# The last four blocks of the down projection in three token parts of 288, 128 and 128 instead of two of 288 and 256

## The chip, the core and the metric

The kernel runs on one core of one Trainium2 chip. The metric is the device time of one execution in microseconds (us), from which a median over runs is taken. A NeuronCore has five engines that each follow their own list of instructions: TensorE (PE in the profile; its weight loads have a row of their own, PEld), VectorE (DVE), ScalarE (ACT), GpSimd (POOL) and SyncE (SP), and 16 DMA engines that move data between the memory of the chip and the on-chip memory. They meet through semaphores.

## What is computed

One inference step of a decoder layer for 512 prompt tokens and 8 x 4 sample tokens, 544 columns in all. Only the end matters here:

```
x = x + (silu(conv) * (u @ w_up)) @ w_down
...
yp = rmsnorm(yp, norm_final)
ys = rmsnorm(ys, norm_final)
```

The rmsnorm divides each token by the root of the mean of its 1024 squares and multiplies by a gain. So no token's output can be formed before all eight row blocks of the down projection have been added for that token.

## The kernel before

Activations lie transposed: 1024 features are 8 tiles `x[m]` (m = 0 to 7, names `xr` in the profile) of 128 partitions, and the 544 tokens are the free dimension. A dense product is done as three products in fp32r (the function `passes`, line 829): every fp32 operand is split into a high and a low part, and high x high, high x low and low x high are added in PSUM. Each of the three has weights of 128 x 128 that are loaded anew. In the feed-forward network the hidden width of 2816 makes 22 blocks; the down projection over blocks 0 to 17 is woven into the products of the gate and the up projection, and blocks 18 to 21 (`DOWN_LAST`, line 39) come at the end, when nothing else is left for TensorE. This end is what the change touches.

There the tokens are cut by `LAST_CUTS` (line 57) in two parts, c = 0 with 288 tokens and c = 1 with 256. `last_half(m, c)` (line 2289) makes one row block m of part c: 4 blocks x 3 products = 12 products into a PSUM tile `ps_dz`, then VectorE adds it to `x[m]`, ScalarE squares the sum, and the square is added to a running sum `acc_final` by GpSimd (m = 1 to 5) or VectorE (m = 6); for m = 0 the square is the running sum's start, and for m = 7 it is kept apart in `sq_last`. For the m in `ON_POOL[c]` ScalarE also multiplies the sum by the gain into `y`. `final(c)` (line 2308) makes the norm of a part: two plain fp32 products with a matrix of ones (`psr_final`) sum the squares over the partitions, ScalarE takes Ln and two Exp (one into PSUM for VectorE, `r_final`; one into `r_fin` for GpSimd), VectorE or GpSimd form eight tiles `y`, and eight DMAs write them out. The order of calls is all of part 0, then part 1 with `final(0)` behind its block m = 2, then `final(1)`.

Nothing is issued as written. The class `Tape` (line 252) records all instructions as steps, and its `order` (line 434) plays them through with its own lengths and lags to fix each engine's list; what stands under `tape.main()` keeps its order on TensorE. PSUM tiles `ps_dz` rotate through three banks (`PF`, line 675), those of the norm through five others (`PX`, line 672). In the profile every recorded compute instruction has line 642, and every DMA line 617, since a helper issues them; the two files differ by one line there, so the changed kernel has 643 and 618.

Of the kernel before, what the change touches and what calls it, by code (L numbers as in the profile page):

```python
# [22 lines left out]
KT = D // 128  # L23
# [9 lines left out]
LN_SET = "natural_log_exp_and_others"  # L33

PLAIN = 4

DOWNS = ((0, 4, 1, (1, 1, 1, 1)), (4, 8, 5, (1, 1, 1, 1)), (8, 12, 9, (1, 1, 1, 1)), (12, 16, 13, (1, 1, 1, 1)),
         (16, 18, 15, (1, 1, 1, 1)))
# [15 lines left out]
LAST_MV = 4  # L54
CUTS = ((0, 256), (256, 288))

LAST_CUTS = ((0, 288), (288, 256))

TILES = (2, 2, 1)
PAIR_LEAD = 10.0  # L60
# [586 lines left out]
def tile_decoder_step(ctx: ExitStack, tc: tile.TileContext, xT, memT, kwT, vw, s0, conv_in, mkT, mv, vecs, cst,  # L647
                      w_first, w_in, w_out, w_cq, w_ck, w_cv, w_co, w_gate, w_up, w_down,
                      yT, kT_out, vT_out, st_out, conv_out, mkT_out, mv_out, ss_out):
    nc = tape = Tape(tc.nc)  # L650
# [9 lines left out]
    def A(name, shape=None, dt=F32):  # L660
        return tape.tile(act, shape or [128, FW], dt, tag="a", name=name, bufs=NA)
# [10 lines left out]
    def PX(name):  # L672
        return tape.tile(psum, [128, 512], F32, tag="aux", name=name, bufs=5)

    def PF(name):

        turn[0] += 1
        return PDEC(name) if turn[0] % 3 == 0 else PD(name)
# [18 lines left out]
    def V(name, i=0):  # L697
        return vec[:, VEC_COLS[name][0] + i:VEC_COLS[name][0] + i + 1]

    def C(name):  # L700
        lo, hi = CST_COLS[name]
        return cs[:, lo:hi] if hi <= mid else cs2[:, lo - mid:hi - mid]
# [13 lines left out]
    ffn_w = len(specs)  # L716
    for j in range(PLAIN):
        specs += [w_gate[j], w_up[j]]
# [110 lines left out]
    def passes(ps, w, xs, n0, n, order, first=True, last=True):  # L829
        for at, i in enumerate(order):  # L830
            (hi, lo), (xh, xl) = w[i], xs[i]
            for j, (a, b) in enumerate(((hi, xh), (hi, xl), (lo, xh))):
                nc.tensor.matmul(ps[:, :n], a, b[:, n0:n0 + n], start=(first and at == 0 and j == 0),
                                 stop=(last and at == len(order) - 1 and j == 2))
# [876 lines left out]
    def add_to(m):  # L1711
        def evac(ps, n0, n):
            nc.vector.tensor_tensor(x[m][:, n0:n0 + n], x[m][:, n0:n0 + n], ps[:, :n], op=ALU.add)
        return evac
# [337 lines left out]
    def down_group(k0, k1, deps):  # L2052

        halves = []
        for m in range(KT):
            k = k1 - k0
            load, box = load_a(f"wd{k0}_{m}", w_down[m][:, 128 * k0:128 * k1].rearrange("p (k c) -> p k c", c=128), k)
            low = split_a(f"wd{k0}_{m}", box, k, load)
            halves += [down_half(k0, k1, m, c, (low, box), deps) for c in range(2)]
        return halves  # L2060
# [163 lines left out]
    gates, hids = {}, {}  # L2224
    for q in range(2 * PLAIN):
        kind, j = "gu"[q % 2], q // 2
# [7 lines left out]
    units = []  # L2234
    for j in range(PLAIN, FT, 2):
        for kind in "gu":
# [3 lines left out]
    downs = [(down_group(k0, k1, [hids[j] for j in range(k0, k1)]), first, each) for k0, k1, first, each in DOWNS]  # L2240
    seq = later.order[:4 * PLAIN]
    seq.insert(-1, units[0].q.pop(1))
# [36 lines left out]
    r_fin, last_sq = A("r_fin"), A("sq_last")  # L2279
    hs, k = [hid[j] for j in range(*DOWN_LAST)], DOWN_LAST[1] - DOWN_LAST[0]  # L2280
    ys = {}
    ON_POOL = (1, 3, 6), (1, 5)

    def y_at(m, c):
        if (m, c) not in ys:
            ys[m, c] = A(f"y{m}_{c}")
        return ys[m, c][:, :LAST_CUTS[c][1]]

    def last_half(m, c):
        n0, n = LAST_CUTS[c]  # L2290
        cut = slice(n0, n0 + n)
        if m == 0 and c == 1:
            tape.gate_at = len(tape.mains) - 1
            nc.sync.dma_start(conv_out, last2)
            nc.scalar.preload_act_table_set(LN_SET)
            tape.gate_at = None
        ps = PF(f"ps_dz{m}_{c}")
        with tape.main():
            passes(ps, held[m], hs, n0, n, range(k))
        add_to(m)(ps, n0, n)  # L2300
        if m < KT - 1:
            ssq3.add(x[m][:, cut], n0, nc.vector if m == KT - 2 else None)
        else:
            nc.scalar.activation(last_sq[:, cut], x[m][:, cut], AF.Square)
        if m in ON_POOL[c]:
            nc.scalar.activation(y_at(m, c), x[m][:, cut], AF.Copy, scale=V("norm_final", m))

    def final(c):
        n0, n = LAST_CUTS[c]
        cut = slice(n0, n0 + n)  # L2310
        ps = PX(f"psr_final{c}")
        for i, sq in enumerate((ssq3.acc, last_sq)):
            nc.tensor.matmul(ps[:, :n], C("ones"), sq[:, cut], start=i == 0, stop=i == 1)
        nc.scalar.activation(r_fin[:, cut], ps[:, :n], AF.Ln, bias=eps, scale=1.0 / D)

        r = PX(f"r_final{c}")[:, :n]
        nc.scalar.activation(r, r_fin[:, cut], AF.Exp, scale=-0.5)
        nc.scalar.activation(r_fin[:, cut], r_fin[:, cut], AF.Exp, scale=-0.5)
        for m in range(KT):
            out = y_at(m, c)  # L2320
            if m in ON_POOL[c]:
                nc.gpsimd.tensor_tensor(out, out, r_fin[:, cut], op=ALU.mult)
            else:
                nc.vector.scalar_tensor_tensor(out, x[m][:, cut], V("norm_final", m), r, op0=ALU.mult, op1=ALU.mult)
            (nc.scalar if c and m % 2 else nc.sync).dma_start(yT[128 * m:128 * m + 128, cut], out)

    held = []
    for m in range(KT):
# [5 lines left out]
            nc.vector.tensor_tensor(lo, t, hi.bitcast(F32), op=ALU.subtract)  # L2334
        held.append([(hi[:, i, :], lo[:, i, :]) for i in range(k)])
        last_half(m, 0)
    for m in range(KT):
        last_half(m, 1)
        if m == 2:
            with tape.main():  # L2340
                final(0)
    with tape.main():
        final(1)
    tape.run()


# [72 lines left out]
```

## Time and profile before

| | us |
|---|---|
| median of 3 runs | 826.87 (825.66 to 828.18) |
| the profiled execution's own time | 827.21 |
| its span, first to last instruction | 825.4 |
| TensorE busy in it | 813.9 (99%) |
| last product of the down projection starts | 816.45 |

The span is what the trace shows; some 1.8 us of the execution's time lie around it. Times in the trace count from the start of the span. TensorE's matmuls are pipelined: a row's duration (0.28 us for a product of 256 columns) is longer than the distance to the next one (0.12 us), and only the distances add up to time. The profile writes fp32r matmuls as f32 with x1 per product, and a plain fp32 product as two rows (x2), one per pass.

### The profile page before, as it was taken

How to read it: one execution, taken by the hardware profiler on the slowest of the kernel's cores; microseconds unless marked ns; L12 is line 12 of the kernel's file. 1: busy time of each engine (PE TensorE's matmuls, PEld its weight loads, DVE VectorE, ACT ScalarE, POOL GpSimd, SP SyncE). 2: the span in 40 equal slices, each digit the busy share in tenths (PEclk: the TensorE clock that was granted, in tenths of full speed). 3: DMA queues.
4: the chain of work that ended last, by engine and by line, in shares of the span. 5: the costliest groups of instructions: out<-in, count | busy, mean ns of one | idle time of the engine just before them, and what ended most of it. 6: DMA issues, size and time to landing. Idle time of an engine off the chain costs nothing.

```text
span 825.4 us, 18881 instructions
## 1 busy us (share of the span) xinstructions
PE 813.9 (99%) x7551; PEld 762.4 (92%) x7551; DVE 617.2 (75%) x1316; ACT 419.0 (51%) x835; POOL 148.0 (18%) x239
## 2 busy tenths in 40 slices
PE   9999999999999999999999999999999999999996
PEld 9999877887888889999889998999999999999995
DVE  6987889866879887564576998976777677767754
ACT  7643455434458345444545456554554455545533
POOL 0030211110210200222323131121112111211013
PEclk9999999999999999999999999999999999999999
DMA  9439999557823444260721347456456645653503
GB/s 343 156 121 297 352 287 304 166 170 226 289 81 110 158 145 153 59 218 31 256 86 53 103 103 203 130 131 176 118 140 181 139 116 145 163 149 83 164 1 109
DMA packets 90759, 132.32 MB, mean 160 GB/s; under 512 B 6064, under 2 KB 60080, under 8 KB 90544
## 3 DMA queue, kind: packets, MB, share of 16 engines
q1 hardware_dynamic: 84480, 120.69, 45.8%
q0 software_dynamic: 5184, 9.44, 7.2%
q8 instruction: 59, 0.97, 0.5%
q10 hardware_dynamic: 1008, 0.99, 0.4%
q14 instruction: 28, 0.23, 0.1%
HBM read 123.03 MB, written 8.07 MB: 159 GB/s over the span
## 4 chain that ended last, share of the span: by engine, by line
PE 91%; DVE 3%; ACT 2%; DMA 2%; issue 0%; SPq 0%; DVEq 0%; ACTq 0%
PE ps_d L642 13%; PE ps_au L642 6%; PE ps_ag L642 6%; PE ps_wo L642 6%; PE ps_cu L642 3%; PE ps_cg L642 3%; PE ps_z_v L642 3%; PE ps_co L642 3%; PE ps_g L642 3%; PE ps_cq L642 3%; PE ps_dz L642 3%; PE ps_u L642 3%; PE ps_z_g L642 2%; PE ps_z_i L642 2%; PE psdo L642 2%; PE psd L642 2%
## 5 line engine op out<-in xcount | busy, mean ns | idle before, releaser
L642 ACT CAST wh<-wr 128x1024 fp32r<-128x1024 f32 (+1 forms) x60 | 52.5, 889 | 73.6 <-issue 12.9
L642 DVE TENSOR_TENSOR wl<-wr,wh 128x1024 fp32r<-128x1024 f32 (+1 forms) x60 | 63.1, 1064 | 9.2 <-ACT wh L642 8.6
L642 DVE TENSOR_TENSOR xr<-xr,ps_d 128x256 f32<-128x256 f32 x80 | 34.5, 434 | 37.6 <-PE ps_d L642 37.5
L642 POOL COPY last<-ug 128x2 f32<-128x2 f32 (+1 forms) x44 | 14.7, 366 | 160.9 <-DVE ug L642 133.9
L642 DVE SCALAR_TENSOR_TENSOR cv<-ug,vec,cv 128x560 f32<-128x560 f32 x44 | 35.1, 798 | 8.1 <-ACT cv L642 7.8
L642 POOL TENSOR_TENSOR hG<-hG,z_f 128x256 f32<-128x256 f32 (+1 forms) x21 | 18.9, 899 | 118.9 <-DVE kq L642 63.5
L642 ACT ACTIVATE cv<-cv 128x560 f32<-128x560 f32 x22 | 14.8, 673 | 19.9 <-DVE cv L642 19.9
L642 ACT ACTIVATE cv<-ug,vec 128x560 f32<-128x560 f32 x22 | 18.8, 856 | 10.6 <-DVE ug L642 9.7
L617 POOL DMA_DIRECT2D S1u<-in_w_up x9 | 7.8, 862 | 89.4 <-DMA S1u<-in_w_up 45.3
L642 ACT ACTIVATE P<-P,mx 128x128 f32<-128x128 f32 (+3 forms) x32 | 17.7, 553 | 11.9 <-DVE mx L642 11.8
L642 POOL TENSOR_TENSOR acc_cx<-acc_cx,sq_cx 128x256 f32<-128x256 f32 (+1 forms) x14 | 11.4, 819 | 59.1 <-ACT sq_cx L642 59.0
L642 POOL COPY ug<-conv_state 128x16 f32<-128x16 f32 x22 | 18.4, 837 | 4.9 <-PE ps_u L642 2.8
L642 PE MATMUL ps_co<-coh,wh 128*128 128x256 f32 (+1 forms) x64 | 19.0, 297 | 0.0
L642 PE MATMUL ps_co<-coh,wl 128*128 128x256 f32 (+1 forms) x64 | 18.4, 288 | 0.0
L642 PE MATMUL ps_co<-col,wh 128*128 128x256 f32 (+1 forms) x64 | 18.4, 288 | 0.0
L642 POOL COPY qbd_win<-z_q 64x32 f32<-64x32 f32 x8 | 8.2, 1024 | 51.1 <-DVE z_q L642 50.9
L642 DVE TENSOR_TENSOR xr<-xr,ps_wo 128x256 f32<-128x256 f32 (+1 forms) x16 | 6.8, 435 | 13.9 <-PE ps_wo L642 13.8
L642 PE MATMUL psdo<-st,dpt 128*32 128x256 f32 x224 | 16.4, 386 | 0.0
L642 DVE TENSOR_TENSOR xr<-xr,ps_dz 128x288 f32<-128x288 f32 (+1 forms) x16 | 7.0, 436 | 12.3 <-PE ps_dz L642 12.3
L642 POOL TENSOR_TENSOR acc_ux<-acc_ux,sq_ux 128x256 f32<-128x256 f32 (+1 forms) x14 | 11.7, 834 | 20.9 <-ACT sq_ux L642 20.8
L642 PE MATMUL psd<-st,qbd_win 128*32 128x224 f32 x256 | 15.3, 358 | 0.0
L642 ACT ACT_TABLE_LOAD x11 | 14.1, 1283 | 2.3 <-issue 2.2
(3122 smaller groups left out, 3635.0 us busy)
## 6 DMA issues: line engine op xcount, KB each, us to landing
st<-in_kwT SPq DMA_DIRECT2D x32, 448.0 KB, 6.2
st<-in_vw SPq DMA_DIRECT2D x28, 512.0 KB, 5.7
wr<-in_w_in SPq DMA_DIRECT2D x17, 512.0 KB, 6.4
wd<-in_w_down SPq DMA_DIRECT2D x32, 256.0 KB, 2.8
wrg<-in_w_gate SPq DMA_DIRECT2D x9, 512.0 KB, 5.9
wru<-in_w_up SPq DMA_DIRECT2D x9, 512.0 KB, 4.6
st<-in_mkT SPq DMA_DIRECT2D x8, 512.0 KB, 6.8
wr<-in_w_out SPq DMA_DIRECT2D x8, 512.0 KB, 3.8
```

The costliest lines, as they stand in the source:

```text
L617: return tape.put(engine, lambda: call(*args, **kw), outs, ins, 0.1, 0.3, size)
L642: return tape.put(engine, lambda: call(*args, **kw), outs, ins, length, lag, size, port, words)
```

## The change

`LAST_CUTS` gets three parts: 288, 128 and 128 tokens. Part c = 1 and part c = 2 are each made of eight row blocks, and `final(c - 1)` follows block m = 2 of part 1 and block m = 4 of part 2 (`FINAL_AT`); `final(2)` is the last. `ON_POOL` gets a middle entry, and the outputs of the odd m of the last part alone go through ScalarE's DMA queue, so that the eight of the middle part go through SyncE's.

```diff
--- before.py
+++ after.py
@@ -33,6 +33,7 @@
 LN_SET = "natural_log_exp_and_others"
 
 PLAIN = 4
+FINAL_AT = 2, 4
 
 DOWNS = ((0, 4, 1, (1, 1, 1, 1)), (4, 8, 5, (1, 1, 1, 1)), (8, 12, 9, (1, 1, 1, 1)), (12, 16, 13, (1, 1, 1, 1)),
          (16, 18, 15, (1, 1, 1, 1)))
@@ -54,7 +55,7 @@
 LAST_MV = 4
 CUTS = ((0, 256), (256, 288))
 
-LAST_CUTS = ((0, 288), (288, 256))
+LAST_CUTS = ((0, 288), (288, 128), (416, 128))
 
 TILES = (2, 2, 1)
 PAIR_LEAD = 10.0
@@ -2279,7 +2280,7 @@
     r_fin, last_sq = A("r_fin"), A("sq_last")
     hs, k = [hid[j] for j in range(*DOWN_LAST)], DOWN_LAST[1] - DOWN_LAST[0]
     ys = {}
-    ON_POOL = (1, 3, 6), (1, 5)
+    ON_POOL = (1, 3, 6), (1, 4, 6), (1, 5)
 
     def y_at(m, c):
         if (m, c) not in ys:
@@ -2322,7 +2323,7 @@
                 nc.gpsimd.tensor_tensor(out, out, r_fin[:, cut], op=ALU.mult)
             else:
                 nc.vector.scalar_tensor_tensor(out, x[m][:, cut], V("norm_final", m), r, op0=ALU.mult, op1=ALU.mult)
-            (nc.scalar if c and m % 2 else nc.sync).dma_start(yT[128 * m:128 * m + 128, cut], out)
+            (nc.scalar if c == 2 and m % 2 else nc.sync).dma_start(yT[128 * m:128 * m + 128, cut], out)
 
     held = []
     for m in range(KT):
@@ -2334,13 +2335,14 @@
             nc.vector.tensor_tensor(lo, t, hi.bitcast(F32), op=ALU.subtract)
         held.append([(hi[:, i, :], lo[:, i, :]) for i in range(k)])
         last_half(m, 0)
-    for m in range(KT):
-        last_half(m, 1)
-        if m == 2:
-            with tape.main():
-                final(0)
+    for c in (1, 2):
+        for m in range(KT):
+            last_half(m, c)
+            if m == FINAL_AT[c - 1]:
+                with tape.main():
+                    final(c - 1)
     with tape.main():
-        final(1)
+        final(2)
     tape.run()
```

How this moves the instructions is seen in each engine's list. First TensorE before, at the end of the program: `ps_dz_1_...` are PSUM tiles of part 1 (the last number is the buffer's), `h21h` and `h21l` the parts of the hidden block, `wdhz`, `wdlz` those of the weights, `psr_final` the sum of squares.

```order
L642 MATMUL ps_dz_1_2030<-h21h,wdlz_1997 128x256
L642 MATMUL psr_final_2032<-acc_final,cs 128x288
L642 MATMUL psr_final_2032<-sq_last,cs 128x288
L642 MATMUL ps_dz_1_2039<-h18h,wdhz_2001 128x256
...
L642 MATMUL ps_dz_1_2048<-h21h,wdlz_2024 128x256
L642 MATMUL psr_final_2049<-acc_final,cs 128x256
L642 MATMUL psr_final_2049<-sq_last,cs 128x256
```

And TensorE's list at the same place in the changed kernel.

```order
L643 MATMUL ps_dz_1_2030<-h21h,wdlz_1997 128x128
L643 MATMUL psr_final_2032<-acc_final,cs 128x288
L643 MATMUL psr_final_2032<-sq_last,cs 128x288
...
L643 MATMUL ps_dz_2_2058<-h21h,wdlz_2008 128x128
L643 MATMUL psr_final_2060<-acc_final,cs 128x128
L643 MATMUL psr_final_2060<-sq_last,cs 128x128
L643 MATMUL ps_dz_2_2067<-h18h,wdhz_2012 128x128
...
L643 MATMUL ps_dz_2_2072<-h21h,wdlz_2024 128x128
L643 MATMUL psr_final_2073<-acc_final,cs 128x128
L643 MATMUL psr_final_2073<-sq_last,cs 128x128
```

Before, 8 x 12 products of 256 columns followed part 0; now 16 x 12 products of 128 columns do, with as many weight loads, and one more pair `psr_final` stands between the fifth and the sixth block of the last part.

Second, VectorE at the end of the changed kernel, from the sixth block of the last part on (`xr` is the addition to `x[m]`, `y_1` and `y_2` are outputs of the middle and the last part).

```order
L643 TENSOR_TENSOR xr_884<-xr_884,ps_dz_2_2067 128x128
L643 SCALAR_TENSOR_TENSOR y_1_2062<-xr_879,vec,r_final_2061 128x128
L643 SCALAR_TENSOR_TENSOR y_1_2063<-xr_881,vec,r_final_2061 128x128
L643 SCALAR_TENSOR_TENSOR y_1_2064<-xr_882,vec,r_final_2061 128x128
L643 TENSOR_TENSOR xr_885<-xr_885,ps_dz_2_2070 128x128
L643 SCALAR_TENSOR_TENSOR y_1_2065<-xr_884,vec,r_final_2061 128x128
L643 SCALAR_TENSOR_TENSOR y_1_2066<-xr_886,vec,r_final_2061 128x128
L643 TENSOR_TENSOR xr_886<-xr_886,ps_dz_2_2072 128x128
L643 TENSOR_TENSOR acc_final<-acc_final,sq_final_6_2071 128x128
L643 SCALAR_TENSOR_TENSOR y_2_2075<-xr_879,vec,r_final_2074 128x128
```

The five outputs of the middle part that VectorE makes stand ahead of the last two additions; before, all six of the last part came after them, 256 wide. Outside the end the planner's run differs in three places by a swap of neighbours (for one, two `psr_hg` products on TensorE).

## The prediction

> **What bounds the kernel now.** I read the page first: busy shares and the chain that ended last.
>
> ```profile
> PE 813.9 (99%) x7551; PEld 762.4 (92%) x7551; DVE 617.2 (75%) x1316; ACT 419.0 (51%) x835; POOL 148.0 (18%) x239
> PE 91%; DVE 3%; ACT 2%; DMA 2%; issue 0%; SPq 0%; DVEq 0%; ACTq 0%
> ```
>
> TensorE is busy for 99% of the span and carries 91% of the chain, so a product added anywhere before the last one moves the end by its full spacing. The end itself is another stage. The view by windows, cut at the moments that the timeline gives, shows it (columns: window, length, busy time and count of PE, PEld, DVE, ACT, POOL, granted clock, DMA share, GB/s).
>
> ```profile
> 804.24:808.50 4.26, 4.26 (x39) 4.26 (x38) 1.49 (x4) 1.77 (x5) 0.27 (x1) 1.00 0.01 4
> 808.50:809.58 1.08, 1.08 (x7) 0.87 (x6) 0.42 (x1) 0.42 (x2) 0.46 (x1) 1.00 0.00 0
> 809.58:816.57 6.99, 6.99 (x61) 6.95 (x59) 3.96 (x10) 3.48 (x9) 5.21 (x7) 1.00 0.49 169
> 816.57:819.36 2.79, 1.56 (x6) 0.59 (x4) 0.61 (x3) 1.28 (x4) 0.00 (x0) 1.00 0.00 0
> 819.36:823.95 4.59, 0.00 (x0) 0.00 (x0) 2.44 (x6) 0.41 (x1) 1.41 (x2) 0.75 0.68 228
> 823.95:825.40 1.45, 0.00 (x0) 0.00 (x0) 0.00 (x0) 0.00 (x0) 0.00 (x0) 0.50 0.00 1
> ```
>
> Up to 816.57 the second part's products run without a gap on TensorE at clock 1.00; then 8.83 us follow (825.40 - 816.57): 2.79 for the norm, 4.59 for outputs and their transfers, 1.45 of closing. The change shortens pieces of the 8.83 and doubles the number of products ahead of it. So two prices decide: a product of 128 columns, and the tail.
>
> **The products.** TensorE's timeline gives the spacing (start, duration, then the instruction):
>
> ```profile
> 802.66 0.29 PE L642 MATMUL ps_dz<-h18h,wdhz 128*128 128x288 f32 x1
> ...
> 804.24 0.28 PE L642 MATMUL ps_dz<-h18h,wdhz 128*128 128x256 f32 x1
> ...
> 808.50 0.65 PE L642 MATMUL psr_final<-acc_final,cs 128*128 128x288 f32 x2
> ...
> 816.45 0.28 PE L642 MATMUL ps_dz<-h21h,wdlz 128*128 128x256 f32 x1
> ```
>
> Twelve products of 288 columns take 804.24 - 802.66 = 1.58 us, 0.132 each; 36 of 256 take 808.50 - 804.24 = 4.26, 0.118 each. Were 128 columns priced by that slope (0.42 ns a column), one would cost 0.065. But each product also loads its 128 x 128 weights, and here 4.26 us of PE hold 4.26 us of PEld: the loads run all the time, hidden behind the columns. What a load costs when nothing hides it is seen where very few columns pass:
>
> ```profile
> 303.47 1.94 PE L642 MATMUL psds<-cs,domn 128*128 128x16 f32 x16
> 422.55 1.85 PE L642 MATMUL ps_cos<-cs,com 128*128 128x16 f32 x16
> L642 PE MATMUL psds<-cs,domn x16: 262/262/263, 303.5 to 305.1; 128*128 128x16 f32 x16
> L642 PEld LDWEIGHTS psds<-cs,domn x16: 192/192/192, 303.4 to 305.1; 128*128 128x128 f32 x16
> L642 PEld LDWEIGHTS ps_dz<-h18h,wdhz x16: 187/188/192, 791.4 to 815.0; 128*128 128x128 f32 x16
> L642 PEld LDWEIGHTS psO<-PT,vt x160: 132/137/138, 136.2 to 281.5; 128*64 128x64 f32 x160
> ```
>
> Sixteen passes with only 16 columns span 1.94 and 1.85 us; less the last one's 0.262 that is 15 distances of 0.112 and 0.106 us. Sixteen columns cannot fill that; the weights do. These are plain fp32 weights; for fp32r the trace has no product under 256 columns, so its price at 128 must be bounded. A load of fp32r weights is recorded with 188 ns, the fp32 one with 192, one of half as many weight columns with 137: the fp32r load looks like the full fp32 one. The lower bound is the slope's 0.065 (no load price at all); the upper one, if loads bind, is the 0.118 of today, behind which a load already fits. I take **0.110**, the middle of the two fp32 rows, to which the recorded load times are nearest.
>
> [...]
>
> Sum on TensorE from 804.24 on. Before: 8 x 12 x 0.1184 = 11.37, and `psr_final` of part 0 with 0.96 (12.33 = 816.57 - 804.24, less 11.37). After: 16 x 12 x 0.110 = 21.12, the same 0.96, and one more pair `psr_final` of 128 columns, four fp32 passes of 0.11 = 0.44 (at most the 0.96 of the wide one). That is 22.52 against 12.33: **+10.19 us**.
>
> Waits do not come on top. A PSUM bank is free again when VectorE has added its block; TensorE gives it 1.32 us per block, close to the 1.42 of now, and VectorE is busy for 3.96 of 6.99 us in the third window. The new `psr_final` pair is queued ahead of three blocks, but its sums are due long before: the middle part ends five blocks, 6.6 us, earlier, and the square and addition chain behind the last block takes about 1.2 us now (816.57 to 817.69 in the tail below).
>
> **The middle part's norm and output.** After that pair, three blocks or 3.96 us of products remain. In them VectorE has five `y_1`, three or four additions, ScalarE an Ln, two Exp and four to five squares or copies, GpSimd four operations. Rows of 128 columns, GpSimd's 256-wide additions, and SyncE's issues:
>
> ```profile
> L642 DVE SCALAR_TENSOR_TENSOR hst<-hst,ftots,psu 128x128 f32<-128x128 f32 x32 | 8.7, 343 | 0.5 <-PE psu L642 0.5
> L642 DVE TENSOR_TENSOR htm<-htm 128x128 f32<-128x128 f32 x4 | 1.2, 289 | 0.1
> L642 POOL TENSOR_TENSOR acc_final<-acc_final,sq_final 128x256 f32<-128x256 f32 x5 | 3.7, 734 | 6.2 <-ACT sq_final L642 6.2
> L617 SPq DMA_DIRECT2D out_yT<-y x12: 332/390/414, 811.2 to 821.5; - x12
> ```
>
> VectorE: 5 x 0.343 + 4 x 0.289 = 2.9 us, under 3.96. Four GpSimd operations of half the width are below 4 x 0.734 = 2.9. So this work is covered; its eight DMA issues on SP (0.4 each, 3.2 us) end about 827.2, and the last part's first output comes near 829. It costs nothing; if the cover were gone, see the last rival.
>
> **The tail.** What follows the last product before the change, behind one row of part 0 at 288 columns:
>
> ```profile
> 804.98 0.45 ACT L642 ACTIVATE sq_last<-xr 128x288 f32<-128x288 f32 x1 [0.61 <-DVE xr L642]
> ...
> 816.77 0.42 DVE L642 TENSOR_TENSOR xr<-xr,ps_dz 128x256 f32<-128x256 f32 x1
> 817.23 0.42 ACT L642 ACTIVATE sq_last<-xr 128x256 f32<-128x256 f32 x1 [1.00 <-DVE xr L642]
> 817.69 0.30 PEld L642 LDWEIGHTS psr_final<-sq_last,cs 128*128 128x128 f32 x2 [0.59 <-ACT sq_last L642]
> 818.43 0.47 ACT L642 ACTIVATE r_fin<-psr_final,eps 128x256 f32<-128x256 f32 x1 [0.79 <-PE psr_final L642]
> 818.94 0.39 ACT L642 ACTIVATE r_final<-r_fin 128x256 f32<-128x256 f32 x1
> 819.36 2.44 DVE L642 SCALAR_TENSOR_TENSOR y<-xr,vec,r_final 128x256 f32<-128x256 f32 x6 [2.17 <-ACT r_final L642]
> 820.65 1.86 ACTq L617 DMA_DIRECT2D out_yT<-y  x4
> ```
>
> At half the width the addition saves 0.13 (0.42 to 0.289); the square, Ln and Exp 0.12 each, from ScalarE's 0.45 at 288 and 0.42 at 256 columns, 0.94 ns a column; and the fp32 pair `psr_final` 0.21 (two passes of 0.21, each to 0.11). The norm's 2.79 become 2.09: -0.70. The six outputs start 0.392 apart ((2.44 - 0.48) / 5); at 343 ns instead of 480 they come 0.255 apart, so the last ends 0.82 earlier. Its transfer still needs an issue and a landing, which fall with the bytes only in part: I take -1.0 for the whole output phase (0.82, and a little of the landing). The lower bound is no gain there; the upper one is half of the 4.59, as half the bytes move. The tail saves **1.7 us**, between 0.7 and 3.0.
>
> **Sum.** +10.19 - 1.7 = +8.5 on the profiled execution's 827.21 gives **835.7 us**. The median of the runs shown, 826.87, lies 0.34 under that execution, which goes into the range, as do the planner's swaps elsewhere. Of these the one on TensorE is at `psr_hg`, whose row
>
> ```profile
> L642 PE MATMUL psr_hg<-hsq,cs x16: 379/444/687, 160.0 to 308.9; 128*128 128x288 f32 x8, 128*128 128x256 f32 x8
> ```
>
> shows sixteen passes of about 0.4 us; a swap of two is worth at most one of them, 0.4 either way, and I put it at nothing.
>
> **The rivals.**
>
> *The load does not bind (not slower).* If fp32r weights arrive quicker than fp32 ones, a product of 128 columns costs the slope's 0.065: 192 x 0.065 = 12.5, +1.1 on the products, +0.44, -1.7: -0.2, or 827.0. It decides at 192 s + 0.44 - 1.7 = 11.37, so at a spacing of s = 0.066: below it the change gains, above it loses. For it: the loads are hidden at 256, and no row shows an unhidden fp32r load. Against it: the recorded 188 ns. Chance 0.10, of which 0.01 for the upper part of its interval, where it is more than 0.3% slower.
>
> *Narrow fp32r runs like fp32.* No row here has fp32r under 256 columns; should it fall back to two passes, its price is that of a plain fp32 product of 128 columns:
>
> ```profile
> 180.69 0.39 PE L642 MATMUL pso<-z_Q,hS 128*128 128x128 f32 x2
> 180.91 0.39 PE L642 MATMUL pso<-hAT,hvt 128*128 128x128 f32 x2
> ```
>
> 0.22 for two passes. 192 x 0.22 = 42.2 instead of 11.37, +0.44 - 1.7: +29.6, or 856.8. For it only the absence of narrow rows; against it that all fp32r products are recorded as one pass with one load. Chance 0.07.
>
> *The middle part is not hidden.* If its outputs are still being issued when the last part's come, SP's four last issues wait for up to the eight's 3.2 us; from a lateness of 2 us (829 - 827) they would start to, and the price is at most half the output phase, 2.3 us: 838.0. Against it the 2 us of slack. Chance 0.02.
>
> **How the numbers follow.** Forecast 0.80, the load free 0.10, the fp32 price 0.07, the middle exposed 0.02, and 0.01 left for a gain, which no pair of bounds gives (a free load with 3.0 saved in the tail is -1.4, or 825.8). Bounds of the forecast: spacing 0.106 with a tail saving of 3.0 gives 20.35 + 0.44 - 11.37 - 3.0 = +6.4, or 833.6; spacing 0.118 with 0.96 for the pair and 0.7 saved gives 22.66 + 0.96 - 11.37 - 0.7 = +11.6, or 838.8. With 0.34 and the swaps: **833.0 to 839.0**, which the exposed middle (838.0) also falls in; together 0.82. Within 0.3% (2.5 us, about what a measurement of this kernel can tell from no change) lies only the free load: 0.09. Faster 0.01, slower 0.90.
>
> **What would show it.** Twelve products `ps_dz` of 128 columns should take 1.3 us (0.8 says the load is free, 2.6 says fp32). The last product should start near 826.7 instead of 816.45. From its end to the span's end there should be about 7.1 us instead of 8.83, and `y_1` work should lie wholly before it. The forecast is wrong if the spacing is under 0.09 or over 0.13, or if the tail grows.

## The result and the profile after

The changed kernel takes **837.17 us** (median of 6 runs, 834.92 to 839.56), the kernel before 827.28 beside it (6 runs, 825.66 to 830.16): a ratio of 1.0117, 95% interval 1.0101 to 1.0133. It is slower, by 9.9 us; 835.7 was forecast. The profiled execution took 837.17 with a span of 835.4, so that 1.8 us lie around the span, as before.

The page of the changed kernel, busy shares and shares of the chain:

```profile
PE 824.1 (99%) x7651; PEld 773.3 (93%) x7651; DVE 618.6 (74%) x1330; ACT 421.8 (50%) x849; POOL 149.6 (18%) x247
PE 91%; DVE 3%; ACT 2%; DMA 2%; issue 0%; SPq 0%; DVEq 0%; ACTq 0%
```

The shares say nothing of the change: TensorE stays at 99% and at 91% of the chain. Its busy time does: 824.1 against 813.9, +10.2 us for exactly 100 more products recorded (96 in `ps_dz`, four passes of `psr_final`). TensorE's timeline of the end places them (start, duration, instruction):

```profile
804.97 0.22 PE L643 MATMUL ps_dz<-h18h,wdhz 128*128 128x128 f32 x1
805.03 0.27 PE L643 MATMUL ps_dz<-h18l,wdhz 128*128 128x128 f32 x1
805.14 0.28 PE L643 MATMUL ps_dz<-h18h,wdlz 128*128 128x128 f32 x1
...
806.26 0.27 PE L643 MATMUL ps_dz<-h18h,wdhz 128*128 128x128 f32 x1
...
823.31 0.44 PE L643 MATMUL psr_final<-acc_final,cs 128*128 128x128 f32 x2
...
823.87 0.27 PE L643 MATMUL ps_dz<-h18l,wdhz 128*128 128x128 f32 x1
...
827.66 0.27 PE L643 MATMUL ps_dz<-h21h,wdlz 128*128 128x128 f32 x1
828.52 0.49 PE L643 MATMUL psr_final<-acc_final,cs 128*128 128x128 f32 x2 [0.58 <-DVE acc_final L643]
```

The first block of part 1 starts at 804.97 and the last product at 827.66; that one ends at 827.77, when the next would have come. This stage lasts 22.80 us where it lasted 12.33. The second narrow product comes 0.06 us after the first; from the third on the distance is 0.11, like that of the weight loads (PEld has them at 804.97, 805.08 and 805.19). What each engine does in it, by windows (columns as in the prediction):

```profile
804.97:808.94 3.97, 3.97 (x39) 3.97 (x37) 1.23 (x4) 1.49 (x5) 0.43 (x1) 1.00 0.02 4
810.02:822.07 12.05, 12.05 (x110) 12.05 (x109) 4.62 (x14) 4.72 (x14) 4.94 (x9) 1.00 0.29 99
823.97:827.95 3.98, 3.96 (x36) 3.82 (x35) 1.87 (x7) 1.96 (x7) 2.19 (x5) 1.00 0.18 51
827.95:829.98 2.03, 0.71 (x4) 0.52 (x4) 0.49 (x2) 0.96 (x4) 0.00 (x0) 1.00 0.45 130
829.98:835.40 5.42, 0.00 (x0) 0.00 (x0) 1.64 (x6) 0.31 (x1) 0.87 (x2) 0.75 0.38 110
```

Products and loads fill the first windows to the end, with no wait between them and the clock at 1.00. The tail, from 827.77 to 835.40, is 7.63 us instead of 8.83 (the trace gives spans to 0.1 us, so tails hold to about 0.05). So the execution's 10.0 us are +10.47 for the products, -1.20 for the tail, and +0.73 from ahead of part 1, which began at 804.97 instead of 804.24.

### The profile page after: what moved, and what is told of

The parts are those of the page before. It is cut to its first block, busy times and chain, and to the rows that moved or that the text cites. A ratio compares the mean times of both kernels' runs of the same rounds, so it can differ in the third digit from the quotient of the medians.

```text
span 835.4 us, 19148 instructions
## 1 busy us (share of the span) xinstructions
PE 824.1 (99%) x7651; PEld 773.3 (93%) x7651; DVE 618.6 (74%) x1330; ACT 421.8 (50%) x849; POOL 149.6 (18%) x247
## 4 chain that ended last, share of the span: by engine, by line
PE 91%; DVE 3%; ACT 2%; DMA 2%; issue 0%; SPq 0%; DVEq 0%; ACTq 0%
PE ps_d L643 13%; PE ps_au L643 6%; PE ps_ag L643 6%; PE ps_wo L643 6%; PE ps_dz L643 4%; PE ps_cu L643 3%; PE ps_cg L643 3%; PE ps_z_v L643 3%; PE ps_co L643 3%; PE ps_g L643 3%; PE ps_cq L643 3%; PE ps_u L643 3%; PE ps_z_g L643 2%; PE ps_z_i L643 2%; PE psdo L643 2%; PE psd L643 2%
## 5 line engine op out<-in xcount | busy, mean ns | idle before, releaser
L643 DVE TENSOR_TENSOR xr<-xr,ps_dz 128x128 f32<-128x128 f32 (+1 forms) x24 | 8.2, 343 | 22.4 <-PE ps_dz L643 22.4
L643 POOL TENSOR_TENSOR acc_final<-acc_final,sq_final 128x128 f32<-128x128 f32 (+1 forms) x15 | 8.6, 575 | 43.3 <-ACT sq_final L643 43.3
```

The lines of the kernel that those rows point to most:

```text
L643: return tape.put(engine, lambda: call(*args, **kw), outs, ins, length, lag, size, port, words)
```

## The experiments

My theory was that the load of fp32r weights sets the pace: at 128 columns a product costs what its 128 weight columns take to load, about 0.11 us. Its rivals: the columns alone are slow at that width (fp32r at a lower rate when narrow, or a fixed floor per instruction), or the time lies in the middle part's norm and outputs.

**Half the weight columns.** With all else of the changed kernel, eleven of a block's twelve narrow products take 64 of the 128 weight columns, so the kernel leaves out a part of the sums for the later tokens.

```diff
-            passes(ps, held[m], hs, n0, n, range(k))
+            (passes if c == 0 else half_passes)(ps, held[m], hs, n0, n, range(k))
...
+                m = 128 if at == 0 and j == 0 else 64
+                nc.tensor.matmul(ps[:m, :n], a[:, :m], b[:, n0:n0 + n], start=(at == 0 and j == 0),
```

> The changed kernel, but eleven of each block's twelve products of 128 columns use only 64 of the 128 weight columns (rows 64 to 127 of the down projection's last four blocks are left out for tokens 288 to 543). Three theories of the 0.111 us per product. Loads bind: the load of half as many weight columns takes about half, so the spacing falls to what 128 token columns cost by the slope of the wide products, 0.065 us, and the 192 products take about 13 instead of 21.4 us. Half rate: fp32r under 256 columns streams at about 0.87 ns per column whatever the weights, spacing stays 0.111. Floor: every narrow product costs a fixed 0.111, spacing stays 0.111. Time: 829 if loads bind, 837 under both others.

A single execution took 829.04 us, against a median of 837.17 for the changed kernel; the products' stage, from 805.36 to the end of the last one, fell from 22.80 to 13.8 us. TensorE in the first two blocks of part 1:

```profile
805.36 0.22 PE L643 MATMUL ps_dz<-h18h,wdhz 128*128 128x128 f32 x1
805.42 0.22 PE L643 MATMUL ps_dz<-h18l,wdhz 128*64 128x128 f32 x1
805.48 0.22 PE L643 MATMUL ps_dz<-h18h,wdlz 128*64 128x128 f32 x1
...
806.09 0.27 PE L643 MATMUL ps_dz<-h18h,wdhz 128*128 128x128 f32 x1
...
806.87 0.27 PE L643 MATMUL ps_dz<-h18h,wdhz 128*128 128x128 f32 x1
```

The moving operand has 128 columns in every row; only `128*128` has become `128*64`. A product then comes 0.06 us after the one before (805.42 to 805.48), and a block takes 806.87 - 806.09 = 0.78 us instead of 1.34. So neither a lower rate of narrow fp32r nor a floor of 0.11 us sets the pace of the changed kernel: at its 128 weight columns the load binds, with 0.11 us. With 64 it costs 0.06 us or less; whether it or the 128 token columns then set the 0.06 isn't shown.

**Parts of 288, 192 and 64.** The same number of loads, with the columns divided differently; if loads alone count, nothing may change.

```diff
-LAST_CUTS = ((0, 288), (288, 128), (416, 128))
+LAST_CUTS = ((0, 288), (288, 192), (480, 64))
```

> The changed kernel with parts of 288, 192 and 64 tokens: as many products as before the edit, other widths. Loads bind: 0.111 us per product in both parts, 1.34 us per block of twelve, since both widths lie under the some 240 columns at which columns and load cost the same. Half rate: 0.167 for 192 columns and 0.056 for 64. Columns alone: 0.092 and 0.038. Total: products unchanged by 0.3 under loads and half rate, the tail some 0.5 us shorter than with 128 (half of the 1.2 us that 256 to 128 saved), so about 836.5, within 1 us of the changed kernel, 1.1% over before.

The time is 844.53 us (ratio 1.0214, interval 1.0185 to 1.0243), 8 us over what my theory expected. TensorE's timeline shows where:

```profile
803.48 0.25 PE L643 MATMUL ps_dz<-h18h,wdhz 128*128 128x192 f32 x1
...
804.80 0.27 PE L643 MATMUL ps_dz<-h18h,wdhz 128*128 128x192 f32 x1
...
816.43 0.28 PE L643 MATMUL ps_dz<-h18h,wdhz 128*128 128x64 f32 x1
...
817.77 0.28 PE L643 MATMUL ps_dz<-h18h,wdhz 128*128 128x64 f32 x1
...
819.11 0.29 PE L643 MATMUL ps_dz<-h18h,wdhz 128*128 128x64 f32 x1
819.22 0.40 PE L643 MATMUL ps_dz<-h18l,wdhz 128*128 128x64 f32 x1
819.43 0.40 PE L643 MATMUL ps_dz<-h18h,wdlz 128*128 128x64 f32 x1
```

A block of 192 columns and the second and third block of 64 take about 1.33 us each, like one of 128: there the theory holds. Then, 4.1 us after the first narrow product (815.15), the distance doubles from 0.11 to 0.21 us. The windows say why:

```profile
815.15:819.00 3.85, 3.85 (x37) 3.85 (x36) 1.06 (x4) 1.11 (x4) 0.32 (x1) 1.00 0.11 38
819.00:832.97 13.97, 13.97 (x67) 13.97 (x66) 1.43 (x6) 2.64 (x9) 2.96 (x7) 0.51 0.03 8
832.97:842.20 9.23, 1.42 (x6) 1.10 (x5) 2.90 (x12) 1.05 (x4) 0.60 (x2) 0.50 0.37 105
```

The granted clock falls from 1.00 to 0.50 and stays there to the end, although TensorE is never idle. At the rate before the fall, 96 products and the pair would have ended about 11.2 us after 815.15, at 826.3; they end at 832.97. Those 6.7 us and a tail of 9.2 instead of 7.6 account for the 8 us. The theory of the load stands, with the clock as a second price that it did not have. The expected time was missed for that reason.

**Two parts of 416 and 128.** The kernel before, cut so that eight blocks are narrow and no block is added.

```diff
-LAST_CUTS = ((0, 288), (288, 256))
+LAST_CUTS = ((0, 416), (416, 128))
```

> The kernel before with two parts of 416 and 128 tokens: only half of the changed kernel's narrow products, and the same last part. Loads bind: 96 x (0.186 + 0.111) = 28.5 us of products against 24.0 before, +0.4 for the wider fp32 sums of the first norm, -1.2 in the tail: +3.7 us, about 831, 0.4 to 0.5% slower than before. If the price lay in anything that a third part brings (its norm pair, its DMAs, the order) and not in narrow products, 96 x (0.186 + 0.065) = 24.1 and the tail's gain would leave it at 826 to 827, no slower than before.

It takes 832.66 us (ratio 1.0066, interval 1.0044 to 1.0087). A block of 416 columns takes 2.27 us, one of 128 again 1.34:

```profile
793.77 0.35 PE L642 MATMUL ps_dz<-h18h,wdhz 128*128 128x416 f32 x1
796.05 0.35 PE L642 MATMUL ps_dz<-h18h,wdhz 128*128 128x416 f32 x1
...
813.23 0.28 PE L642 MATMUL ps_dz<-h18h,wdhz 128*128 128x128 f32 x1
814.57 0.28 PE L642 MATMUL ps_dz<-h18h,wdhz 128*128 128x128 f32 x1
...
823.90 0.28 PE L642 MATMUL ps_dz<-h21h,wdlz 128*128 128x128 f32 x1
825.31 0.49 PE L642 MATMUL psr_final<-acc_final,cs 128*128 128x128 f32 x2 [1.14 <-DVE acc_final L642]
```

From the first product at 793.77 to the span's end at 832.0 are 38.2 us; before, 791.55 to 825.4, 33.85: +4.4 for the end, where 3.7 was expected, and the rest from ahead of it. Of the 0.7 that were not expected, 0.3 are the wide products and 0.3 the tail: its last pair waits 1.14 us for `acc_final`. Saving the third part does not help, since the 128 columns still cost a full load (0.1115 us) while 416 cost 0.189 each; at 0.065, the price by the columns alone, the 96 narrow products would have taken 96 x 0.0465 = 4.5 us less, about the loss of the end.

**No outputs of the middle part.** The changed kernel without the eight DMAs of part 1, whose 128 tokens are not written out.

```diff
-            (nc.scalar if c == 2 and m % 2 else nc.sync).dma_start(yT[128 * m:128 * m + 128, cut], out)
+            if c != 1:
+                (nc.scalar if c == 2 and m % 2 else nc.sync).dma_start(yT[128 * m:128 * m + 128, cut], out)
```

> The changed kernel without the eight DMAs that write the middle part (its 128 tokens of the output are left out; the norm and the products for it stay). If the middle part's output is hidden, as predicted: the stretch from the last product's end to the span's end stays at 7.6 us within 0.2, and the time at the changed kernel's within 1 us. If its issues or transfers hold up the last part's: that stretch falls by 0.5 to 2.3 us and the time with it.

It takes 836.79 us (836.12 to 838.37), within the spread of the changed kernel. Its end:

```profile
828.75 0.27 PE L643 MATMUL ps_dz<-h21h,wdlz 128*128 128x128 f32 x1
...
831.96 2.07 ACTq L618 DMA_DIRECT2D out_yT<-y  x4
```

The tail, from 828.86 to the span's 836.6, is 7.74 us, no shorter than 7.63. The middle part's DMAs are hidden here; that rival falls.

**Parts of 304 and 240.** From the widths so far, by an estimate, the columns begin to count at about 240, where both prices meet (0.0109 us + 240 x 0.42 ns = 0.1117, the load 0.1115). The kernel before at that point:

```diff
-LAST_CUTS = ((0, 288), (288, 256))
+LAST_CUTS = ((0, 304), (304, 240))
```

> The kernel before with parts of 304 and 240 tokens. If a product costs the larger of its columns (0.0109 + 0.00042 n us) and its load (0.1115), 240 columns are where the two meet (0.1117), and nothing is lost yet: 96 x (0.1386 + 0.1117) = 24.03 us of products against 24.0 before, 0.05 more for the first norm, 0.1 to 0.2 less in the tail. Within 0.1% of before. If the load cost more than 0.1115 when it is not hidden, or the narrow part's blocks left the adding engines behind, up to 1 us slower.

It takes 827.16 us beside 827.17 for the kernel before (ratio 1.0001, interval 0.9987 to 1.0015): no difference. Its blocks:

```profile
794.34 0.30 PE L642 MATMUL ps_dz<-h18h,wdhz 128*128 128x304 f32 x1
796.02 0.30 PE L642 MATMUL ps_dz<-h18h,wdhz 128*128 128x304 f32 x1
...
809.07 0.28 PE L642 MATMUL ps_dz<-h18h,wdhz 128*128 128x240 f32 x1
810.42 0.28 PE L642 MATMUL ps_dz<-h18h,wdhz 128*128 128x240 f32 x1
```

A block of 240 columns takes 1.35 us, like one of 64, 128 or 192, and 304 take 1.68. No cut tried here beats the kernel before.

**Both kernels again**, for the 0.73 us ahead of part 1: one more profile of each, with nothing edited.

> The kernel before, for one more trace. The first product of the last blocks started at 791.5 in the first trace of before and between 790.8 and 793.8 in the traces with other ends. If that spread is from execution to execution, this one lies in it too, with a wait of TensorE for h3h of 0 to 1.5 us; if the changed order of instructions ahead of the end causes it, it is at 791.5 within 0.3.

> The changed kernel, for one more trace. The first product of the last blocks started at 792.2 in its first trace. By chance: anywhere between 790.5 and 794. In any case 22.8 us from the first narrow product to the last one's end, and 7.6 us behind it.

They took 825.72 and 837.05 us. The stage of the products lasts 12.34 and 22.81 us, the tail 8.82 and 7.67: these hold within 0.05. What lies ahead does not. The first product `ps_dz` came at 791.55 and 790.06 before, and at 792.25 and 792.10 after. Two places far upstream show why, in windows of the kernel before and of the changed one, in the first profiles:

```profile
300.00:310.00 10.00, 10.00 (x57) 8.69 (x56) 7.01 (x19) 4.83 (x12) 0.00 (x0) 0.83 0.42 113
500.00:512.00 12.00, 10.50 (x78) 9.70 (x77) 8.75 (x17) 7.32 (x14) 3.17 (x8) 1.00 0.78 188
```

```profile
300.00:310.00 10.00, 10.00 (x63) 8.82 (x62) 7.90 (x22) 5.50 (x15) 0.00 (x0) 1.00 0.41 113
500.00:512.00 12.00, 10.03 (x64) 9.07 (x63) 7.32 (x12) 7.21 (x14) 2.89 (x7) 0.86 0.63 161
```

Near 300 to 310 us the clock dips in three of the nine profiles; near 500 to 512 TensorE waits for 1 to 3 us, and in three the clock dips behind that wait. Idle time there, plus what a clock under 1.00 takes, sums to 1.7 + 1.5 = 3.2 us before and 2.0 + 12 x 0.14 = 3.7 after; 1.0 in the second profile of before; 1.5 in the second one of the changed kernel, with another 1.3 waited near 100 to 200; 5.1 without the middle part's outputs and 5.4 with 304 and 240. Taken off the start of the products in each of the nine profiles, such sums leave 788.4, 789.1, 788.9 and 789.6 for the kernels in two parts, and 788.6, 789.4, 788.3, 789.4 and 789.8 for those in three. So the two orders do not differ ahead of the end by more than the executions do.

No run was made to find why a given execution dips, but the traces show when. In all nine, every change of the granted clock lies a whole number of steps of 3.41 us behind its first rise (88, 89 and 239 steps in the first profile of the kernel before, 146, 147 and 242 in that of the changed one); a dip ahead of the end lasts one step, in the profile of 304 and 240 two. The kernel before, by such steps:

```profile
302.82:306.23 3.41, 3.41 (x26) 3.23 (x27) 2.32 (x6) 1.48 (x5) 0.00 (x0) 1.00 0.58 118
306.23:309.64 3.41, 3.41 (x10) 2.70 (x9) 1.88 (x4) 1.90 (x5) 0.00 (x0) 0.50 0.64 214
309.64:313.05 3.41, 3.41 (x16) 2.75 (x16) 2.30 (x6) 3.38 (x10) 0.00 (x0) 1.00 0.00 0
```

TensorE has no gap ahead of this dip; what lies there are the sixteen passes `psds` of 16 columns (at 303.47). The dip comes in the three profiles in which a step ends 0.8 to 1.2 us after the last of these passes starts, and not in the six in which it ends 1.4 to 2.4 us after. Near 500 to 512 it comes behind the three steps in which TensorE waited 1.6 to 1.8 us, and behind none there with 1.56 or less. So what goes with the dip in these nine is where the steps lie, which differs between executions, and how long TensorE waits in one; dips are seen in kernels with either order.

## Why the prediction was right

**The products: right.** The forecast rested on 0.110 us a product, from the nearest rows of fp32 loads; it is 0.1115 (1.34 us for twelve). That makes 192 x 0.0015 = 0.29 us more, all of the gap between the 22.52 forecast for the stage and the 22.80 measured. That loads set this pace is shown by the half weights. That it is the pace of fp32 loads was concluded from recorded durations of 188 and 192 ns, which say that the loads are alike, but are longer than what either costs. The two rows behind the choice gave 0.106 and 0.112, so the closeness of 0.110 is in part luck.

**The extra pair: right.** `psr_final` between the fifth and sixth block cost 0.45 us: 823.87 - 823.20, the start of the product ahead of it, is 0.67, less two distances of 0.11. The forecast said 0.44.

**The tail: right in its sign, too large.** 1.20 us were saved, not 1.7, though within the bounds of 0.7 to 3.0. The norm and the outputs, in rows of the changed kernel:

```profile
827.97 0.29 DVE L643 TENSOR_TENSOR xr<-xr,ps_dz 128x128 f32<-128x128 f32 x1 [0.53 <-PE ps_dz L643]
828.18 0.28 DVE L643 TENSOR_TENSOR acc_final<-acc_final,sq_final 128x128 f32<-128x128 f32 x1
...
829.27 0.37 ACT L643 ACTIVATE r_fin<-psr_final,eps 128x128 f32<-128x128 f32 x1 [0.66 <-PE psr_final L643]
829.67 0.28 ACT L643 ACTIVATE r_final<-r_fin 128x128 f32<-128x128 f32 x1
829.98 1.64 DVE L643 SCALAR_TENSOR_TENSOR y<-xr,vec,r_final 128x128 f32<-128x128 f32 x6 [1.52 <-ACT r_final L643]
830.88 2.07 ACTq L618 DMA_DIRECT2D out_yT<-y  x4
```

The norm took 829.98 - 827.77 = 2.21 us, a saving of 0.58 against 0.70 forecast: its first pair, at 828.52, waits for `acc_final`, which VectorE adds only behind the last `xr`. The output phase fell from 6.04 to 5.42, by 0.62 against 1.0. The term that was mis-sized is this phase: I let VectorE's pace set it (0.82 us, and its six outputs do take 0.80 less). But ScalarE's queue begins its four issues 0.90 us after `r_final` instead of 1.29 (-0.39), needs 2.07 from the first issue to the last one's end instead of 1.86 (+0.21), and the rest to the span's end is 2.45 instead of 2.89 (-0.44). Half the bytes did not halve an issue: the four take 0.34 to 0.40 us each, before 0.35 to 0.41. The +0.21 lies between them: one starts 0.39 us after the end of the issue ahead of it (at 832.11), where the others follow after 0.1 or less. What it waited for isn't shown; the gap is there without the middle part's outputs too.

**The middle part: hidden, but with less to spare.** VectorE's outputs of it end before the last product does; SyncE's issues for them do not:

```profile
825.50 0.86 DVE L643 SCALAR_TENSOR_TENSOR y<-xr,vec,r_final 128x128 f32<-128x128 f32 x3
...
825.87 3.65 SPq L618 DMA_DIRECT2D out_yT<-y  x8
...
826.84 0.60 DVE L643 SCALAR_TENSOR_TENSOR y<-xr,vec,r_final 128x128 f32<-128x128 f32 x2
```

VectorE is done at 827.44. The eight issues end at 829.52 instead of 827.2 as forecast, 1.75 us after the last product, and the last part's first issue comes at 830.36: 0.84 us were left of the 2 counted on. They lie behind the last part's norm, and leaving out the DMAs gained nothing.

**The rivals.** The free load (827.0) needed 0.065 us a product, fp32's price (856.8) 0.22; the rows have 0.1115. The distance was 111 ns with 128 weight columns; with 64, in the run with half the weight columns, it was 61, which shows only that such a load costs no more than that.

**Ahead of the end.** The swaps elsewhere were put at nothing, within 0.4 us either way. Of the +0.73 that the first pair of profiles shows, the dips and waits above explain about 0.5; the rest lies within the spread of the executions. The forecast erred by 1.5 us in all: 0.73 ahead of part 1, 0.28 for the products, 0.5 for the tail.

## What to carry to other kernels

In these runs, at a granted clock of 1.00, a product in fp32r that loads its own 128 weight columns cost the larger of the load, 0.1115 us, and its moving columns. The widths of 256 and 288 give 0.0109 us + 0.42 ns a column for these (304 and 416, with 0.1395 and 0.189, lie up to 0.004 above), so below about 240 columns, by that estimate, every further cut of this part adds a full load per product (here 96 x 0.1115 = 10.7 us) and saves nothing per product: blocks of 240, 192 and 128 took 1.35, 1.33 and 1.34 us. Splitting the last part to shorten a tail pays only if the tail saves more than the loads that it adds, and here halving the last part's tokens saved 1.2 us of 8.83: the issues hardly got shorter with the bytes (0.34 to 0.40 us, before 0.35 to 0.41), and the rest behind them fell from 2.89 to 2.45 us only. When a bottleneck engine is at 99%, read the distance between its instructions, not its share.

## What the runs showed of the hardware unexpectedly

The granted clock fell to 0.50 after 4.1 us of products with 64 columns behind loads of 128 weight columns, without an idle moment on TensorE; with 128 columns per load it stayed at 1.00 for 23 us. At 0.50 the distance set by the load nearly doubled too, from 0.1115 to 0.213 us. The 4.1 us need be no fixed delay: the clock fell at 819.24, at the end of the first of the 3.41 us steps that held 64-column products alone (815.83 to 819.24). As this stream had no gap, the fall did not come behind a wait of TensorE. That it came from the few moving columns of such a step (some 31 products of 64 by their distance, where the changed kernel's steps have as many of 128) is my reading, which no run of its own tested. The dips near 306 us, behind passes of 16 columns and without a gap, fit it; of the narrow products of the end, only widths of 64 and more were run, and no run set out to find the limit.
